# A decoder layer on eight cores: the last down pass by token quarters over a bf16 weight copy, four K heads first, and GpSimd work tied to a mask

## The chip, the cores and the metric

The kernel runs as one program on the 8 cores of one Trainium2 chip: cores 0 to 3 are one die, 4 to 7 the other. The metric is device time in microseconds (us) of the slowest core. Most runs of a kernel agree within 0.3%. Some runs fall into a slower state, in which one die or both get a lower TensorE clock; each run is labelled fast or slow, and only fast runs are compared here. The experiments ran on several chips, each beside the kernel before on the same chip.

Engine names in the profile: PE is TensorE, PEld its weight loads, DVE is VectorE, ACT is ScalarE, POOL is GpSimd, SP is SyncE. "L474" is line 474 of that kernel, so that one operation has different line numbers in different kernels.

## The reference, cut to what matters

One hybrid decoder layer, 16384 tokens, width 2048, float32 in and out:

```python
proj = x @ w_in + b_in                       # Q, K, V of group A; Q, K, V of group B
ya = dilated_mixture_attention(rope(qa), rope(ka), va)   # group A: 8 heads, three dilation patterns
yb = sink_window_attention(rope(qb), rope(kb), vb, sinks) # group B: 16 heads, 2 KV heads, window 128
y = concat([rms_norm(ya, g_a), rms_norm(yb, g_b)]) @ w_out
x = layer_norm(ALPHA * x + y, ln1_g, ln1_b)
x = layer_norm(ALPHA * x + (silu(gate) * up) @ w_down, ln2_g, ln2_b)   # d_ff = 5632
```

Each core computes 2048 tokens. It projects K and V for these tokens and the 2048 before them, stores them to memory, then projects Q and does the attention, then the rest.

## The kernel before

The phases follow each other on TensorE: K and V of eight x tiles of 512 tokens; Q and the attention of group B; that of group A; the output projection; and, for each half of 1024 tokens, an up pass and a down pass. Weights and x are loaded by GpSimd's DMA queue, which casts float32 to bf16. Three places matter here.

The start computes V of the first tile as its weights arrive, then V of the second tile, then K head by head. SyncE's queue loads the rope tables and V's bias at once, without a wait.

In the attention loops, VectorE's rope operations for later Q tiles stand in a queue (`dveq`, four to a tile), and `run(dveq, n)` puts n of them between the masks.

```python
for u in range(32):            # group B
    b_PV(j, kq, pend); b_evac(j, kq)
    run(peq, 1)
    proj(u + LEAD)             # the next Q projection, into one of two PSUM banks
    run(dveq, 4)               # its rope
    if u >= 29: reduce_b(u - 29)     # RMS statistics, into one of the same two banks
...
for u in range(32):            # group A
    for p_ in range(3):        # three dilation patterns
        spend.append(a_S(...)) # scores, exp (ScalarE), mask (VectorE)
        run(dveq, 2 if p_ == 0 else 1)
        a_PV(...)              # (cut: half of the next projection, before the third pattern's a_PV)
        if u >= 29 and p_ == 1: reduce_a(u - 29)   # needs acc of the block
    a_evac(h, c)               # output multiply (VectorE), copy and acc (GpSimd)
    proj(u + 32 + LEAD, 1)     # its other half
```

The down pass takes each weight tile for both token quarters of 512, so both sets of LayerNorm statistics are complete only at its end:

```python
for si in range(2 * KC):
    n, hh = si // 2, si % 2        # weight tile n, quarter hh
    ...                            # 44 matmuls, residual add, stats(n, hh, z, ...)
finish(0, 4); finish(1, 6)         # statistics of both quarters, then 32 tiles to normalise
```

The softmax here doesn't subtract the row's maximum and nothing guards it: scores larger than these inputs give would overflow.

Of the kernel before, what the change touches and what calls it, by code (L numbers as in the profile page):

```python
# [203 lines left out]
def build(debug=False):  # L204
# [15 lines left out]
    k.wk_d = ein("wk", [8, 128, KC, 128])  # L220
# [16 lines left out]
    k.rb_d = dt("rb", [128, TOK], F32, kind="Internal").ap()  # L237
    k.x1s_d = dt("x1s", [KC, 128, TOK], F32, kind="Internal").ap()
# [44 lines left out]
def persist(k):  # L283
    nc, S_ = k.nc, k.S
    P = Place(k, 0, 8192)
    k.perm, k.bperm = P("perm", 128)
    k.ones, k.bones = P("ones", 128)
    k.onh, k.bonh = P("onh", 128)
    k.onesf, k.bonesf = P("onesf", 128, F32)
    k.bqk, bs = P("bqk", 25, F32)  # L290
    k.bsmall = bs
    k.bsw, _ = P("bsw", 16, F32)
    k.gmix, _ = P("gmix", KC, F32)
    lnp, _ = P("lnp", 4 * KC, F32)
    k.lnp = lnp.rearrange("p (a b) -> p a b", a=4)
    k.esink, _ = P("esink", 8, F32)
    k.p_end = P.o
    S_.dma("pool", k.perm, k.perm_d, [], [k.bperm], "perm")
    for v, d in ((k.bqk, k.bqk_d), (k.bsw, k.bsw_d), (k.gmix, k.gmix_d), (k.lnp, k.lnp_d), (k.esink, k.sinks_d)):
        S_.dma("sp", v, d, [], [], "small", joins=[bs])  # L300
    S_.dve(lambda: nc.vector.memset(k.ones, 1.0), [], [k.bones])
    S_.dve(lambda: nc.vector.memset(k.onesf, 1.0), [], [k.bonesf])
    S_.act(lambda: nc.scalar.activation(out=k.esink, in_=k.esink, func=AF.Exp), [bs], [bs])
    S_.dve(lambda: nc.vector.tensor_scalar(out=k.gmix, in0=k.gmix, scalar1=32.0, scalar2=None, op0=ALU.mult), [bs], [bs])
# [46 lines left out]
def phase1(k):  # L351
# [9 lines left out]
    wk, bwk = [], []  # L361
    for h in range(8):
        v, b = P("wk%d" % h, KC * 128)
        wk.append(v.rearrange("p (a b) -> p a b", a=KC))
        bwk.append(b)
# [13 lines left out]
    ct = {"bk": 0, "t": 0, "ko": 0, "vo": 0}  # L379
# [21 lines left out]
    s0 = xs[slot_of[0]]  # L401
    bl0 = []
    kc = 0
    for p_ in (1, 1, 2, 4, 4, 4):
        o_ = XO + kc * 1024
        b_ = S_.buf("x0_%d" % kc, o_, o_ + p_ * 1024)
        S_.dma("pool", s0[:, kc:kc + p_, :], k.xT_d[0, :, kc:kc + p_, :], [], [b_], "x0_%d" % kc)
        bl0 += [b_] * p_
        for q in range(kc, kc + p_, 2):
            n_ = min(2, kc + p_ - q)  # L410
            for q_ in range(q, q + n_):
                S_.dma("pool", wv[:, q_, :], k.wv_d[q_], [], [bwv[q_]], "wv%d" % q_)
        kc += p_
    bx[0] = bl0
    S_.dma("sp", bv, k.bv_d[0], [], [bbv], "bv")
# [3 lines left out]
    load_x(1, (4, 4, 4, 4))  # L419
    for h in range(8):  # L420
        S_.dma("pool", wk[h], k.wk_d[h], [], [bwk[h]], "wk%d" % h)
    S_.dma("pool", wkb, k.wkb_d, [], [bwkb], "wkb")
# [38 lines left out]
    def k_tile(t, h):  # L461
        x = xs[slot_of[t]]
        bk = nx("bk", 8)
        ri = t % 2

        def mm():
            for kc in range(KC):
                ins = nc.tensor.matmul(bank(k, bk), wk[h][:, kc, :], x[:, kc, :], start=(kc == 0), stop=(kc == KC - 1))  # L468
            return ins
        S_.pe(mm, bx[t] + [bwk[h]], [k.bBK[bk]])  # L470
        flush()
        ti = nx("t", 2)
        ko, bko = KO[ki := nx("ko", 3)]
        rope_a(k, bk, h, ra[ri][:, 0, :], ra[ri][:, 1, :], bra[ri], T1[ti][0], T1[ti][1], T2[ti][0], T2[ti][1], ko, bko)  # L474
        b = Buf("ka%d_%d" % (h, t))
        S_.dma("sp", k.ka_d[h, t], ko, [bko], [b], "ko%d" % ki)
        k.bka[h].append(b)
# [25 lines left out]
    def load_ra(t):  # L503
        S_.dma("sp", ra[t % 2], k.ropeA_d[t], [], [bra[t % 2]], "ra%d" % (t % 2))

    load_ra(0)
    load_ra(1)
    x = xs[0]
    for kc in range(KC):
        def mm(kc=kc):  # L510
            for blk in range(4):
                for g in range(2):
                    ins = nc.tensor.matmul(bank(k, blk * 2 + g), x[:, kc, blk * 128:blk * 128 + 128],
                                           wv[:, kc, g * 512:g * 512 + 512], start=(kc == 0), stop=(kc == KC - 1))
            return ins
        S_.pe(mm, [bx[0][kc], bwv[kc]], k.bBK)
    for blk in range(4):
        v_out(0, blk, [(0, 512), (512, 1024)], [blk * 2, blk * 2 + 1])
    for blk in range(4):
        v_tile(1, blk)  # L520
    for h in range(8):
        k_tile(0, h)
    load_x(2, (8, 8))
    load_ra(2)
    for h in range(8):
        k_tile(1, h)
        if h == 0:
            load_x(3, (8, 8))
    load_ra(3)
# [28 lines left out]
def phase2(k):  # L558
# [312 lines left out]
    def a_evac(h, c):  # L871
# [9 lines left out]
        if h == 0:  # L881
            S_.pool(lambda: nc.gpsimd.tensor_tensor(out=ac, in0=yc, in1=yc, op=ALU.mult), [byc], [bacc[c]])
        else:
            S_.act(lambda: nc.scalar.activation(out=sq, in_=yc, func=AF.Square), [byc], [SQ[1]])
        if h < 7:
            y, by = YA[h % 2]
            if c == 0:
                open_gen(by)
            S_.pool(lambda: nc.gpsimd.tensor_copy(out=res(y), in_=ma(yc)), [byc], [], [by])
        else:  # L890
            for st in range(2):
                S_.pool(lambda st=st: nc.gpsimd.tensor_copy(out=res(k.y[st][:, 7, :]), in_=ma(yc)[:, 64 * st:64 * st + 64]), [byc],
                        [], k.by[st][7])
        if h > 0:
            eng, ve = ("dve", nc.vector) if (h, c) == (7, 3) else ("pool", nc.gpsimd)
            S_._add(eng, lambda: ve.tensor_tensor(out=ac, in0=ac, in1=sq, op=ALU.add), [SQ[1], bacc[c]], [bacc[c]])
        if c == 3 and h < 7:
            b = Buf("ys%d" % h)
            S_.dma("sp", k.ys_d[h], y, [by], [b], "ya")
            k.bys[h] = b  # L900

    rsum = []
# [31 lines left out]
    for u in range(32):  # L934
# [6 lines left out]
        run(peq, 1)  # L941
        proj(u + LEAD)
        run(dveq, 4)
# [6 lines left out]
    for u in range(32):  # L950
# [7 lines left out]
        if u == 28:  # L958
            k.y_load(0, 6)
            k.y_load(1, 6)  # L960
            wfill(k)
        for p_ in range(3):
# [4 lines left out]
            run(dveq, 2 if p_ == 0 else 1)  # L967
# [3 lines left out]
            if 28 <= u < 31:  # L971
                for _ in range(2):
                    if len(k.norms) > 48:
                        out_norm(k, *k.norms.pop(0))
            if u >= 29 and p_ == 1:
# [3 lines left out]
        a_evac(h, c)  # L979
        proj(u + 32 + LEAD, 1)  # L980
# [14 lines left out]
def out_open(k, rsum):  # L995
# [30 lines left out]
    for st in range(2):  # L1026
        k.wlist += [(("u", st, f), k.wup_d[f], KC * 256, KC, ((8192, 16384, 0) if st == 0 else (0, 16384, 8192))[f % 3]) for f in range(FC)]
        k.wlist += [(("d", st, n), k.wdn_d[n], FC * 128, FC, (0, 11264)[n % 2]) for n in range(KC)]
# [3 lines left out]
def wfill(k):  # L1032

    while k.wlist:
# [6 lines left out]
        k.S.dma("pool", v, src, [], [b], "ws")  # L1041
# [30 lines left out]
def phase3(k):  # L1072
# [128 lines left out]
    wdone(k, "xr")  # L1201
    hslots = list(range(32, 44)) + list(range(32))
    zr = {}
    bz2s = {}
    for st in range(2):
# [37 lines left out]
        zring = []  # L1243
        for si in range(2 * KC):
            n, hh = si // 2, si % 2
            if hh == 0:
                w, bw = k.wts[("d", st, n)]
# [13 lines left out]
            if hh == 1:  # L1261
                wdone(k, ("d", st, n))
# [3 lines left out]
                                                                          op1=ALU.add), [bxb, k.bBK[bk]], [bz])  # L1266
            stats(n, hh, z, bz, sqs)
# [4 lines left out]
            zr[(st, n, hh)] = (z, bz)  # L1272
        if st == 0:
            fins += [lambda: finish(0, 6), lambda: finish(1, 6)]
        else:
            finish(0, 4)
            finish(1, 6)

        def ln2_tile(st, n, hh, idx):
            c0 = st * TS + hh * 512  # L1280
            (mu, bmu), (rs, brs) = stat[hh]
            if st == 0:
                z, bz = slot("zl%d" % idx, R[0] + (4 + idx % 6) * 2048)
                S_.dma("sp", z, k.z2s_d[n, :, c0:c0 + 512], [bz2s[(n, hh)]], [bz], "zl%d" % (idx % 6))
            else:
                z, bz = zr[(st, n, hh)]
            eng = S_.dve
            e = nc.vector
            S_.dve(lambda: nc.vector.tensor_tensor(out=z, in0=z, in1=mu, op=ALU.subtract), [bz, bmu], [bz])  # L1289
            S_.dve(lambda: nc.vector.tensor_tensor(out=z, in0=z, in1=rs, op=ALU.mult), [bz, brs], [bz])  # L1290
            S_.act(lambda: nc.scalar.activation(out=z, in_=z, func=AF.Identity, bias=k.lnp[:, 3, n:n + 1], scale=k.lnp[:, 2, n:n + 1]),
                   [bz, k.bsmall], [bz])
            b = Buf("out%d_%d_%d" % (st, n, hh))
            final.append(S_.dma("act", k.outT_d[n, :, c0:c0 + 512], z, [bz], [b], "of%d" % (idx % 6)))

        for hh in range(2):
            for n in range(KC):
                jobs.append(lambda st=st, n=n, hh=hh, idx=hh * KC + n: ln2_tile(st, n, hh, idx))
# [37 lines left out]
def prepare_inputs(x, w_in, b_in, sinks, g_mix_a, g_mix_b, w_out, ln1_g, ln1_b, w_up, w_down, ln2_g, ln2_b):  # L1336
# [11 lines left out]
    wk = chunks(w_in[:, 1024:2048])  # L1348
# [24 lines left out]
    shared = dict(wq=wq, wk=wk, wkb=wkb, wv=wv, bqk=bqk, bsw=bsw, wout=wout, wup=wup, wdn=wdn, gmix=gmix, lnp=lnp,  # L1373
# [35 lines left out]
```

## Time and profile before

| | us |
|---|---|
| median of 4 runs (lowest to highest) | 3147.1 (3145.7 to 3152.4) |
| spans of the profiled run, by core | 3122.0 to 3137.1 |
| TensorE busy, slowest core | 2985.4 |

The profiled run took 3138.2 us, some 8 us less than the four timed ones.

To follow a change through such a kernel, the span is cut at instructions that stay the same. The stages below are read from the first and last TensorE start of certain lines; they are medians over the eight cores, and the last one is measured to the end of the span.

| stage | before, us |
|---|---|
| start, K and V, to the first Q projection | 514.7 |
| group B, to its first statistics matmul | 190.0 |
| to the last Q projection (most of group A) | 232.9 |
| to the first output projection (end of group A) | 50.2 |
| output projection | 238.8 |
| up, down, up (sum of the three) | 1542.9 |
| last down pass | 303.7 |
| tail after the last down matmul | 55.1 |

TensorE's waits before. The columns are: engine and line that waited, what ended the wait, us in total, number of waits, the longest.

```profile
PE sp L846 <- DVE arena L876: 32.5, 27, 3.9
PE sp L513 <- DMA arena<-wv: 21.5, 7, 9.4
PE sp L455 <- DMA arena<-xT: 9.9, 1, 9.9
```

The first line is group A: the next block's output matmuls wait for VectorE to multiply the block before (L876). The other two are the start: V's weights and the second x tile come too late.

TensorE's timeline of the start before, on core 5. The columns are start, us, engine, line, operation, and in brackets the idle time before it and what ended it.

```profile
67.45 30.04 PE L455 MATMUL sp<-arena 128*128 128x512 bf16 x128 [8.45 <-DMA arena<-xT]
97.32 55.42 PE L468 MATMUL sp<-arena 128*128 128x512 bf16 x256
152.57 27.79 PE L455 MATMUL sp<-arena 128*128 128x512 bf16 x128
180.20 27.79 PE L468 MATMUL sp<-arena 128*128 128x512 bf16 x128
```

Before 67.45 us there are another 128 matmuls. So 640 matmuls are done at 180.20. At the steady 0.216 us each (128 in 27.79 us), that is 138 us of work: 42 us are lost.

The end of TensorE's work before, on the slowest core, whose span ends at 3137.1: the last down matmuls end at 3082.6, and only statistics follow.

```profile
3059.78 22.83 PE L1258 MATMUL sp<-arena 128*128 128x512 bf16 x105
3082.44 1.88 PE L1115 MATMUL sp<-arena 128*128 128x512 f32 x4
```

### The profile page before, as it was taken

Reading aid. Unit: us, or ns where it says so; the run is one execution under the profiler, and the core shown is the slowest. Engines: PE = TensorE matmul, PEld = TensorE weight load, DVE = VectorE, ACT = ScalarE, POOL = GpSimd, SP = SyncE. Lnnn points to the kernel's source line nnn. Section 1 sums busy time; section 2 is a strip of 40 time slices with the busy share of each in tenths; the row PEclk is TensorE's granted clock in tenths of the full one; section 3 lists DMA queues with packets and bytes.
Section 4 is the critical chain, followed back from the end, with each engine's and each line's share of the span. In section 5 each row is a group of like instructions: output and inputs, shape, how many; then the busy total and the mean of one; then the engine's idle time right before and its main releaser. Section 6 shows DMA issues by size and latency. Waiting matters only on the chain.

```text
span 3137.1 us, 40048 instructions; the slowest of 8 cores (3122.0 to 3137.1 us)
## 1 busy us (share of the span) xinstructions
PE 2985.4 (95%) x15989; PEld 1423.7 (45%) x15989; DVE 1086.0 (35%) x1452; ACT 643.2 (21%) x889; POOL 594.4 (19%) x598
## 2 busy tenths in 40 slices
PE   5999999999997998999999999999999999999993
PEld 2445554545664443444444444444444444444441
DVE  0555545887776685421001000002420100100006
ACT  0000001665554133310000001112210000011114
POOL 2000000453323966000000002321000000012231
PEclk8999999999999999999999999999999999999997
DMA  9852213255557898754443446667954444445443
GB/s 171 158 120 87 79 52 78 41 124 132 120 132 188 166 195 166 149 102 78 81 76 73 81 86 128 135 128 147 215 106 78 81 72 76 81 85 108 103 104 111
DMA packets 186425, 352.36 MB, mean 112 GB/s; under 512 B 86400, under 2 KB 104064, under 8 KB 169344
## 3 DMA queue, kind: packets, MB, share of 16 engines
q0 software_dynamic: 31536, 190.13, 35.4%
q1 hardware_dynamic: 135696, 125.04, 14.7%
q10 hardware_dynamic: 19008, 34.61, 3.5%
q8 instruction: 129, 2.11, 0.3%
q14 instruction: 56, 0.46, 0.1%
HBM read 471.11 MB, written 68.75 MB: 172 GB/s over the span
## 4 chain that ended last, share of the span: by engine, by line
PE 81%; DVE 7%; DMA 5%; issue 3%; ACT 2%; POOL 1%; another core or an unknown queue 0%; DVEq 0%; ACTq 0%; SPq 0%; POOLq 0%
PE sp L1223 35%; PE sp L1258 19%; PE sp L468 7%; PE sp L455 7%; PE sp L692 4%; PE sp L1066 4%; DMA arena<-z2s 2%; DMA arena<-wv 1%; DMA outT<-arena 1%; DVE arena L655 1%; DVE arena L1130 1%; DVE arena L1290 1%; DVE arena L1289 1%; DVE arena L876 1%; ACT arena L826 1%
## 5 line engine op out<-in xcount | busy, mean ns | idle before, releaser
L1223 PE MATMUL sp<-arena 128*128 128x512 bf16 x5632 | 1223.1, 381 | 12.9 <-DVE arena L1231 7.6
L1223 PEld LDWEIGHTS sp<-arena 128*128 128x128 bf16 x5632 | 551.4, 98 | 685.7 <-issue 25.5
L1258 PE MATMUL sp<-arena 128*128 128x512 bf16 x2816 | 608.1, 379 | 2.2 <-ACT arena L1230 2.2
L1231 DVE TENSOR_TENSOR arena<-sp,arena 128x512 bf16<-128x512 f32 x176 | 121.6, 692 | 982.3 <-ACT arena L1230 982.3
L1258 PEld LDWEIGHTS sp<-arena 128*128 128x128 bf16 x2816 | 275.0, 98 | 335.3 <-issue 3.1
L1230 ACT ACTIVATE arena<-sp 128x512 f32<-128x512 f32 x176 | 105.0, 597 | 925.6 <-PE sp L1223 918.0
L127 POOL DMA_DIRECT2D arena<-wup x88 | 46.6, 530 | 1110.5 <-PE sp L1223 1077.5
L1265 DVE SCALAR_TENSOR_TENSOR arena<-arena,sp 128x512 f32<-128x512 f32 x64 | 44.0, 688 | 565.0 <-PE sp L1258 305.0
L692 PE MATMUL sp<-arena 128*128 128x512 bf16 x1024 | 235.5, 379 | 3.9 <-DVE arena L346 3.9
L1066 PE MATMUL sp<-arena 128*128 128x512 bf16 x1024 | 222.3, 379 | 5.6 <-DVE arena L1185 3.2
L1106 POOL TENSOR_TENSOR arena<-arena 128x512 f32<-128x512 f32 x120 | 158.4, 1320 | 350.3 <-DVE arena L1265 312.2
L455 PE MATMUL sp<-arena 128*128 128x384 bf16 (+1 forms) x1168 | 212.8, 345 | 9.9 <-DMA arena<-xT 9.9
L468 PE MATMUL sp<-arena 128*128 128x512 bf16 x1024 | 222.2, 379 | 0.0
L655 DVE TENSOR_TENSOR arena<-arena 128x1024 bf16<-128x1024 bf16 x160 | 144.3, 916 | 65.3 <-ACT arena L826 54.1
L455 PEld LDWEIGHTS sp<-arena 128*128 128x128 bf16 x1168 | 114.5, 98 | 106.9 <-issue 13.7
L1107 POOL TENSOR_TENSOR arena<-arena 128x512 f32<-128x512 f32 x120 | 160.2, 1335 | 0.0
L1066 PEld LDWEIGHTS sp<-arena 128*128 128x128 bf16 x1024 | 99.6, 98 | 128.4 <-issue 9.5
L468 PEld LDWEIGHTS sp<-arena 128*128 128x128 bf16 x1024 | 100.0, 98 | 120.5
L1105 ACT ACTIVATE arena<-arena 128x512 f32<-128x512 f32 x120 | 75.5, 629 | 363.0 <-DVE arena L1265 267.7
L692 PEld LDWEIGHTS sp<-arena 128*128 128x128 bf16 x1024 | 96.4, 98 | 113.4 <-issue 7.3
L340 ACT ACTIVATE arena<-sp,arena 128x512 bf16<-128x512 f32 (+1 forms) x37 | 25.1, 678 | 564.1 <-PE sp L488 443.6
L437 DVE TENSOR_TENSOR arena<-sp,arena 128x384 bf16<-128x384 f32 (+1 forms) x81 | 47.9, 605 | 200.5 <-PE sp L455 105.4
(102 smaller groups left out, 2012.9 us busy)
## 6 DMA issues: line engine op xcount, KB each, us to landing
arena<-wup POOLq DMA_DIRECT2D x88, 1024.0 KB, 9.0
arena<-wdn POOLq DMA_DIRECT2D x32, 1408.0 KB, 11.7
arena<-wout POOLq DMA_DIRECT2D x32, 512.0 KB, 10.1
arena<-xres SPq DMA_DIRECT2D x64, 256.0 KB, 8.0
x1s<-arena ACTq DMA_DIRECT2D x64, 256.0 KB, 7.7
arena<-x1s SPq DMA_DIRECT2D x64, 256.0 KB, 5.0
outT<-arena ACTq DMA_DIRECT2D x64, 256.0 KB, 4.0
arena<-xT POOLq DMA_DIRECT2D x12, 1024.0 KB, 21.9
```

Of the source, the lines that this page charges most:

```text
L455: ins = nc.tensor.matmul(bank(k, bk)[:, 0:c1 - c0], x[:, kc, blk * 128:blk * 128 + 128], wv[:, kc, c0:c1], start=(kc == 0), stop=(kc == KC ...
L468: ins = nc.tensor.matmul(bank(k, bk), wk[h][:, kc, :], x[:, kc, :], start=(kc == 0), stop=(kc == KC - 1))
L655: S_.dve(lambda: nc.vector.tensor_tensor(out=pg, in0=pg, in1=m.to_broadcast([128, rows, 1024 // rows]), op=ALU.mult), [bp, b], [bp])
L692: ins = nc.tensor.matmul(bank(k, bk), w[:, kc, :], x[:, kc, :], start=(kc == 0), stop=(kc == KC - 1))
L1066: ins = nc.tensor.matmul(bank(k, bk), w[:, kc, :], y[:, kc, hh * 512:(hh + 1) * 512], start=(first and i == 0), stop=(last and i == len(kc ...
L1105: S_.act(lambda: nc.scalar.activation(out=sq, in_=z, func=AF.Square), [bz], [bsq])
L1106: S_.pool(lambda: nc.gpsimd.tensor_tensor(out=za, in0=za, in1=z, op=ALU.add), [bz, bza], [bza])
L1107: S_.pool(lambda: nc.gpsimd.tensor_tensor(out=qa, in0=qa, in1=sq, op=ALU.add), [bsq, bqa], [bqa])
L1223: ins = nc.tensor.matmul(bank(k, a + half), w[:, kc, half * 128:half * 128 + 128], xb[:, kc, hh * 512:(hh + 1) * 512], start=(kc == 0), st ...
L1230: S_.act(lambda si=si, a=a: nc.scalar.activation(out=sg[si][0], in_=bank(k, a), func=AF.Silu), [k.bBK[a]], [sg[si][1]])
L1231: S_.dve(lambda si=si, a=a, f=f, hh=hh: nc.vector.tensor_tensor(out=h[f][:, hh * 512:(hh + 1) * 512], in0=bank(k, a + 1), in1=sg[si][0], o ...
L1258: ins = nc.tensor.matmul(bank(k, bk), w[:, fc, :], h[fc][:, hh * 512:(hh + 1) * 512], start=(fc == 0), stop=(fc == FC - 1))
```

## The change

It has three parts.

1. **Start.** K of four heads is computed first, for two x tiles at once, as x and weights arrive, filling all eight PSUM banks. ScalarE copies the banks into staging buffers so that they come free, and VectorE ropes from there. V follows. The rope tables and V's bias are loaded later, to leave the DMA engines to what comes first.
2. **Group A.** The last rope add moves behind the output multiply. GpSimd's copy and sum are held back until the next block's first mask is done. In group B, rope moves ahead of the next projection. With the last add, the third of the four rope operations moves too, from the second mask to the first.
3. **Down.** The first down pass stores each weight tile once as bf16. The last one goes by quarters, reading the bf16 copy twice, and normalises the first quarter under the second one's matmuls. A shorter end is split over three engines.

The diff, cut to its core (left out, among others: two loads of the output projection's input move one pattern later in block 28 of group A):

```diff
@@ start @@
+    for p_ in (1, 1, 2, 2, 2, 2, 2, 2, 2):        # x of tiles 0 and 1, K weights of four heads, in turn
+        ...
+    for h in range(4, 8): S_.dma("pool", wk[h], ...)
+    for kc in range(KC): S_.dma("pool", wv[:, kc, :], k.wv_d[kc], [], [bwv[kc]], "wv")
+    late = [bx[1][15]]
+    S_.dma("sp", bv, k.bv_d[0], [bwv[8]], [bbv], "bv")     # waits for the ninth part of V's weights
...
+    load_ra(0, late)                                       # rope tables: wait for the last x chunk
+    load_ra(1, late)
+    for kc in range(KC): ...                               # K of heads 0 to 3, tiles 0 and 1
+    for h in range(4):
+        for t in range(2): k_out(t, h, 2 * h + t)          # ScalarE staging, rope, store
@@ group B @@
+        run(dveq, 4)
         proj(u + LEAD)
-        run(dveq, 4)
@@ group A @@
-            run(dveq, 2 if p_ == 0 else 1)
+            if p_ == 0:
+                run(dveq, 3)
+                while poolq:
+                    poolq.pop(0)([spend[-1][1]])           # GpSimd waits for the mask just issued
...
         a_evac(h, c)                                       # now queues its GpSimd work in poolq
+        run(dveq, 1)
@@ down @@
-        for si in range(2 * KC):
-            n, hh = si // 2, si % 2
+        steps = [(n, hh) for n in range(KC) for hh in range(2)] if st == 0 else [(n, hh) for hh in range(2) for n in range(KC)]
+        for si, (n, hh) in enumerate(steps):
...
+            if st == 0 and hh == 0:
+                S_.dma("sp", k.wdb_d[n], w, [bw], [k.bwdb[n]], "wdb")
...
+            if st == 1 and si == 15:
+                fins.append(lambda: finish(0, 6))
+                jobs += [lambda n=n: ln2_tile(1, n, 0, n) for n in range(KC)]
```

## The prediction

> **What bounds it now.** TensorE is busy 2985 of 3137 us on the slowest core (page, part 1). The change goes at three of its gaps. (1) Start: in the timeline the first matmul is at 9.4 us, then it waits for V weights, then 9.9 us for the second x tile; at 68.4 us only 128 matmuls are done, 27.6 us of work at the steady 216 ns. 41 us are lost. (2) Group A (740 to 970 us): TensorE 205.7 of 230 us busy; the waits view gives 32.5 us in 27 waits to VectorE's output multiply. One block lasts 8.2 us. (3) Tail: the last down matmul ends at 3082.5; the remaining 54.5 us are statistics (about 6), 32 tiles on VectorE at 1.40 us, and the last store (2.7).
>
> **Tail.** By quarters, 16 tiles are normalised under the second quarter's matmuls. Left after the last matmul: z 0.9; four f32 matmuls, mean and variance to 5.7; table load 1.28, Ln and Exp to about 9; VectorE 17 passes of 0.69 beside GpSimd 11 of 1.27, to about 23; last ScalarE pass and store to about 28. Saved 26, less 2 for the first quarter's statistics matmuls, now in the TensorE stream: **-24 us**.
> Price: weights are stored once as bf16 (1.44 MB per 19 us, first down pass) and read twice. The DMA view there shows 16% of 16 engines moving 16.3 MB on the hardware queue, so about 4.3 us more per 19, at a share of 0.62 now: 0.84. No stall above a few us. In the second pass each 9.5 us step needs its own 1.44 MB. The skill's "DMA: Bandwidth & Descriptors" (Anatomy of one DMA) fits 2.0 us + bytes/436e3: 5.3 us; this trace has nothing as good (2 MB rope load: 11.4 us under contention). Estimate 6 to 8 us: no stall, little room.
>
> **Start.** K of four heads for two x tiles needs 12.6 MB for 128 matmuls; each 0.79 MB feeds 1.73 us of work. At the trace's rate, about 0.3 MB/us of f32 source, the first stage ends near 50, K of the other heads 78, V weights land near 95. Lost then about 28 instead of 41; ScalarE staging (0.65 per tile) frees the banks, VectorE's rope backlog (2.9 per tile) is absorbed. **-13 us** (8 to 18).
>
> **Group A.** The strided last rope add (1.06 us) stands before the output multiply on VectorE and delays it 0.45 us; it moves behind. Saved 0.4 in 26 blocks. The first mask lasts 1.33 to 1.42 instead of 0.69 while GpSimd copies; the skill ("SBUF — State Buffer", Who interferes with whom) says VectorE with two SBUF inputs contends with GpSimd reads. Tying GpSimd behind the mask restores 0.69, but TensorE rarely waits there (1.5 us). **-11 us**.
>
> **Sum.** 3147 - 48 = **3099 us**, range 3080 to 3122. Faster by over 2% (below 3084) 0.17, within 2% 0.82, slower 0.01.
>
> **Right if:** last down matmul to end 26 to 31 us; TensorE 99% busy in both down passes; first 512 matmuls end near 140, not 153.9 us; block period 7.7 to 7.9 us; first mask 0.69.
> **Wrong if:** bf16 loads land later than 9.5 us (gaps before down steps), bf16 stores delay x1 loads or weights in the first down pass, or V weights come late because K stores and rope tables share the DMA engines; better, if more of group A's 24 idle us goes.

## More of the kernel before

K and V go to memory through small output buffers:

```python
KO = [P("ko%d" % i, 512) for i in range(3)]       # K outputs: three buffers
VO = [P("vo%d" % i, VW) for i in range(2)]        # V outputs: two buffers
...
S_.dma("sp", bv, k.bv_d[0], [], [bbv], "bv")      # V's bias: waits for nothing
...                                               # (cut: load_ra(0), load_ra(1), x and weight loads)
for blk in range(4):
    v_tile(1, blk)
for h in range(8):
    k_tile(0, h)                                  # 16 matmuls, rope on VectorE, store on SyncE's queue
```

## The result, and the profile after

The kernel after is correct. Its median is 3184.95 us (3176.33 to 3190.48, four runs), against 3147.1: ratio 1.0115, 95% interval 1.0089 to 1.0141. A ratio is the mean time of one kernel's fast runs over that of the other's of the same rounds, so it is not quite the ratio of the medians quoted. A gain of 48 us had been predicted; 38 us were lost.

The cores come first, because a die that lost its clock must not be explained as a scheduling effect. The lines for the two dies, before and then after:

```profile
die 0 (median of its cores): 3130.2 us, clock 0.986
die 1 (median of its cores): 3128.2 us, clock 0.985
```

```profile
die 0 (median of its cores): 3157.1 us, clock 0.980
die 1 (median of its cores): 3178.7 us, clock 0.970
```

Die 0 is 27 us longer than before. Die 1 is another 22 us longer at a lower clock: it loses 11 us in the output projection and 6 to 7 us in the first down pass, where die 0 loses nothing. In the trace, cores 4 and 5 were granted a clock of 0.81 for 201 us in all, nearly all of it in short pieces after 1071 us, and cores 6 and 7 for 167 us; cores 0 to 3 never. So the schedule accounts for 27 us, and the rest is a question of clock (run e15 below).

Stages in medians over cores; the two columns on the right are runs of the experiments, which the text comes to.

| stage | before | after, die 0 | after again (e15) | best (e13) |
|---|---|---|---|---|
| start, K and V | 514.7 | 550.8 | 550.0 | 507.6 |
| group B to first statistics | 190.0 | 192.4 | 192.2 | 191.4 |
| to last Q projection | 232.9 | 237.3 | 236.2 | 228.1 |
| end of group A | 50.2 | 60.8 | 60.7 | 52.2 |
| output projection | 238.8 | 238.7 | 239.3 | 238.6 |
| last down pass | 303.7 | 305.4 | 305.4 | 305.4 |
| tail | 55.1 | 29.8 | 29.4 | 29.8 |

The tail gained 25 us as predicted. The start lost 36 us instead of gaining 13, and the group A edits lost 16 to 17 us in the three attention stages, instead of gaining 11.

TensorE's waits after:

```profile
PE sp L552 <- ACT arena L486: 34.4, 1, 34.4
PE sp L880 <- DVE arena L910: 22.5, 16, 5.2
PE sp L535 <- DMA arena<-wka: 19.2, 7, 8.7
PE sp L462 <- DVE arena L444: 9.9, 1, 9.9
PE sp L961 <- DVE arena L328: 7.1, 3, 2.7
PE sp L951 <- POOL arena L932: 6.8, 3, 3.1
```

Group A's known wait fell from 32.5 to 22.5 us (second line; medians over the cores 31.1 and 22.5), so that part of the reasoning worked. But four new waits stand there: one of 34.4 us for ScalarE's staging copy, one of 9.9 us for V's evacuation, and two sets of three in front of the statistics matmuls of group B (L961) and group A (L951).

The start after on core 5: first SyncE's queue, then VectorE's rope, then TensorE.

```profile
78.44 0.33 SPq L127 DMA_DIRECT2D arena<-bv  x1
78.86 1.21 SPq L127 DMA_DIRECT2D arena<-ropeA  x2
```

```profile
99.25 1.39 DVE L492 TENSOR_TENSOR arena<-arena 64x512 f32<-64x512 f32 x2 [88.58 <-DMA arena<-ropeA]
```

```profile
55.01 27.79 PE L474 MATMUL sp<-arena 128*128 128x512 bf16 x128 [1.10 <-ACT arena L486]
117.24 15.42 PE L552 MATMUL sp<-arena 128*128 128x512 bf16 x64 [34.44 <-ACT arena L486]
156.40 58.54 PE L462 MATMUL sp<-arena 128*128 128x512 bf16 x256 [9.94 <-DVE arena L444]
```

TensorE has 256 matmuls done at 82.8 us, where the kernel before had them at 97.3. The plan works up to there. Then it stands still: rope cannot start before 99.25, because the rope table's load was issued only at 78.86 and then took 20 us to land. It stood in SyncE's queue behind V's bias, which waits for a part of V's weights. Without rope, the eight staging buffers stay full, ScalarE can't empty PSUM, and TensorE has no bank. 640 matmuls are done at 214.9 us, 35 us later than before.

The tail after, on core 5, whose span ends at 3182.6: the last down matmuls end at 3153.8.

```profile
3129.79 23.98 PE L1366 MATMUL sp<-arena 128*128 128x512 bf16 x107
3153.61 1.88 PE L1283 MATMUL sp<-arena 128*128 128x512 f32 x4
```

The DMA view after, with KB each and the median us from issue to landing:

```profile
arena<-wdb SPq DMA_DIRECT2D x32, 1408.0 KB, 6.3
arena<-wdn POOLq DMA_DIRECT2D x16, 1408.0 KB, 13.8
wdb<-arena SPq DMA_DIRECT2D x16, 1408.0 KB, 12.5
```

A bf16 weight tile lands 6.3 us after its issue (the median), and TensorE consumes one in 9.5 us. In both down passes together TensorE waits 2.3 us.

### The profile page after: what moved, and what is told of

The parts are those of the page before. It is cut to its first block, busy times and chain, and to the rows that moved or that the text cites. A ratio compares the mean times of both kernels' runs of the same rounds, so it can differ in the third digit from the quotient of the medians.

```text
span 3182.6 us, 40219 instructions; the slowest of 8 cores (3147.1 to 3182.6 us)
## 1 busy us (share of the span) xinstructions
PE 3029.5 (95%) x15993; PEld 1438.0 (45%) x15993; DVE 1078.5 (34%) x1440; ACT 655.7 (21%) x907; POOL 619.6 (19%) x605
## 4 chain that ended last, share of the span: by engine, by line
PE 78%; DMA 10%; DVE 3%; ACT 3%; another core or an unknown queue 2%; issue 2%; POOL 1%; SPq 0%; ACTq 0%; DVEq 0%; POOLq 0%
PE sp L1332 36%; PE sp L1366 10%; PE sp L1120 7%; DMA arena<-x1s 7%; PE sp L462 7%; PE sp L474 5%; PE sp L726 5%; DMA arena<-z2s 1%; DMA arena<-ropeA 1%; PE sp L891 1%; ACT arena L1361 1%; DVE arena L1377 1%; DVE arena L910 1%; ACT arena L908 1%
## 5 line engine op out<-in xcount | busy, mean ns | idle before, releaser
L462 PE MATMUL sp<-arena 128*128 128x384 bf16 (+1 forms) x1232 | 227.4, 347 | 9.9 <-DVE arena L444 9.9
L689 DVE TENSOR_TENSOR arena<-arena 128x1024 bf16<-128x1024 bf16 x160 | 129.7, 836 | 61.3 <-ACT arena L860 45.5
L1361 ACT ACTIVATE arena<-arena 128x512 f32<-128x512 f32 x64 | 52.0, 813 | 362.3 <-DMA arena<-x1s 361.8
L1159 ACT ACTIVATE arena<-arena 128x512 f32<-128x512 f32 x119 | 74.9, 629 | 211.1 <-DVE arena L1377 108.0
```

Source lines behind the costliest of these rows:

```text
L462: ins = nc.tensor.matmul(bank(k, bk)[:, 0:c1 - c0], x[:, kc, blk * 128:blk * 128 + 128], wv[:, kc, c0:c1], start=(kc == 0), stop=(kc == KC ...
L689: S_.dve(lambda: nc.vector.tensor_tensor(out=pg, in0=pg, in1=m.to_broadcast([128, rows, 1024 // rows]), op=ALU.mult), [bp, b], [bp])
L1361: S_.act(lambda xb=xb, n=n: nc.scalar.activation(out=xb, in_=xb, func=AF.Identity, bias=k.lnp[:, 1, n:n + 1], scale=k.lnp[:, 0, n:n + 1]), ...
```

## The experiments

Fifteen experiments were run (e14 repeats the kernel of e10, e15 the kernel after). Some of them were executed only once or twice (e7, e8, e9, e12); those are read by their stages more than by their time.

### The start: is it only the position of V's bias? (e1, e2)

My theory was that the wait of V's bias on V's weights blocks everything behind it in SyncE's queue. The rival was that the DMA engines are simply full.

```diff
 # e1: V's bias behind the rope tables
-    S_.dma("sp", bv, k.bv_d[0], [bwv[8]], [bbv], "bv")
...
     load_ra(0, late)
     load_ra(1, late)
+    S_.dma("sp", bv, k.bv_d[0], [bwv[8]], [bbv], "bv")
 # e2: besides, load_ra(0) and load_ra(1) without the wait
```

> The changed kernel with one line moved: the load of the V bias stands after the two rope tables in SyncE's queue, not before. Theory (in-order queue: the rope tables stand behind the V bias, which waits for a V weight piece that lands only at 78 us): the tables are issued near 50 us, the 34 us wait of TensorE for the ScalarE staging falls to under 10, the first Q projection starts near 515 us instead of 550, the time is about 3150 (3140 to 3160). Rival (the 16 DMA engines are full of weights, so the tables land late wherever they stand): wait still over 20 us, time over 3168.

> The changed kernel with the rope tables loaded at the very start, waiting for nothing, and the V bias after them. In-order theory: no wait of TensorE for the staging is left, the first stage is at most 4 us later, the first Q projection starts at 498 to 508 us, the time is about 3138 (3128 to 3150). Bandwidth rival: the first stage gets slower by over 8 us and eats it, time as for the kernel with the bias last or more.

Measured: e1 has a start of 545.2 us and fast runs at 3160 to 3166; e2 has 545.5 us and fast runs at 3155 to 3180. Against what was expected, the start is 30 us too long in e1 and over 37 in e2. The first block was real: in e1 the tables land 10 and 14 us after their issue, and TensorE's wait for the staging copy falls from 34.4 to 7.6 us (core 5), as the theory said; so full DMA engines were not the main thing that held the tables. But taking the block away showed the next, a TensorE wait of 27.8 us for V's evacuation. SyncE's queue of e1 on core 5:

```profile
49.94 0.96 SPq L127 DMA_DIRECT2D arena<-ropeA  x2
83.37 0.33 SPq L127 DMA_DIRECT2D arena<-bv  x1
83.80 68.95 SPq L127 DMA_DIRECT2D ka<-arena  x16
```

The rope table now goes out at 49.94, but the K stores stand behind the bias and start at 83.80. VectorE fills the three K output buffers and then waits:

```profile
102.80 0.69 DVE L494 TENSOR_TENSOR arena<-arena 128x512 bf16<-128x512 f32 x1 [30.80 <-DMA ka<-arena]
```

The Trainium skill says why the order matters: in "DMA: Bandwidth & Descriptors" (Anatomy of one DMA), "DMA engines do not wait on semaphores"; a wait is done by the issuing sequencer before dispatch. The trace agrees: a queue whose head waited until 83.37 issued nothing behind it before.

### No wait in SyncE's queue at all, and more K buffers (e5, e6)

```diff
 # e5
-    load_ra(0, late); load_ra(1, late)
+    load_ra(0); load_ra(1)
+    S_.dma("sp", bv, k.bv_d[0], [], [bbv], "bv")
 # e6: e5, and K outputs of tiles 0 and 1 in sixteen buffers
+        if t < 2:
+            ki = 3 + nx("kx", 16)
+            ko, bko = KX[ki - 3]
```

> The changed kernel with rope tables and V bias loaded at the start, none waiting: SyncE's queue never blocks. The run with the bias last moved the block from the tables to the K stores (issued at 82 us, 20 us to landing, VectorE stands 31 us). If the queue order is all of it: K stores are issued from about 62 us, VectorE's ropes never stand over 5 us, first Q projection at 500 to 508 us, time about 3125 to 3138 on an undisturbed chip. If the stores themselves are slow while weights fill the 16 engines (20 us each, three output buffers, so 6.7 us a K tile against 3.45 on TensorE): waits of VectorE for K stores go on until about 100 us, TensorE still waits 10 us or more after the first V tiles, first Q projection at 515 to 535 us.

> As e5_sp_free, and each of the first 16 K tiles gets an output buffer of its own, so that no rope waits for a store. If slow stores with three buffers are what is left: VectorE ropes run through (2.95 us each, done near 110 us), TensorE waits for staging or V evacuation under 8 us, first Q projection at 498 to 508 us. If VectorE's rope work itself is too slow for a K-first order, it stays at 515 or more although no rope waits for a store.

Measured: e5 3144.3 us (3140.6 to 3160.6), ratio 1.0031 (0.9953 to 1.0108), start 528.0, as the second expectation had it (slow stores). e6 3144.8 us (the median of four, one of them slow), ratio 1.0011 (0.9979 to 1.0042), start 527.5. So the wait in the queue is worth 22 us of the 36. Sixteen K buffers alone add nothing, though rope now runs through to 109.8 us as expected, because the next thing in line is V. Of e6, core 3, VectorE's evacuation of V:

```profile
149.95 2.48 DVE L444 TENSOR_TENSOR arena<-sp,arena 128x512 bf16<-128x512 f32 x4 [37.77 <-DMA vs<-arena]
```

A V store of 256 KB, issued at 111, had its buffer free only 38 us later. Two rope tables stand just before it in the queue, but they are not the reason: in e13 below they are issued after these V stores, and the first of them still land 30 to 36 us after their issue. There are two V buffers, so VectorE and then TensorE (18.4 us in one wait) stand behind it. Over the window from 60 to 150 us the DMA view of core 5 shows, for K stores (the lines are of the kernel after, then of e5):

```profile
ka<-arena SPq DMA_DIRECT2D x14, 128.0 KB, 1.9
```

```profile
ka<-arena SPq DMA_DIRECT2D x16, 128.0 KB, 10.3
vs<-arena SPq DMA_DIRECT2D x2, 256.0 KB, 23.8
```

The same 128 KB store takes 1.9 us when most of the loads are through, as they were after the stall of the kernel after, and 10.3 us while they run. The skill's fit of 2.0 us plus bytes over 436e3 (same page, same section; made for GpSimd's queue) gives 2.3 us for it, an estimate. The trace is near it for the unloaded store; the other took more than four times as long.

### More V buffers (e9), and the same without the losses of group A (e10, e11)

```diff
 # e9: the rope tables, then the bias, wait for the last x chunk only; eight V buffers
-    S_.dma("sp", bv, k.bv_d[0], [bwv[8]], [bbv], "bv")
+    S_.dma("sp", bv, k.bv_d[0], late, [bbv], "bv")
-        vi = nx("vo", 2)
+        vi = 2 + nx("vx", 8) if t < 2 else nx("vo", 2)
     # and the rope tables of tiles 2 and 3 are loaded after V of tile 1
```

> The kernel after, with the rope tables and then the values' bias waiting only for the last chunk of the first x (not for the last part of the values' weights), with eight output buffers for the values of the first two row groups instead of two, and the third and fourth rope tables loaded later. Theory (small stores wait 20 to 40 us behind large loads, and too few output buffers hand that wait to VectorE and TensorE): the first K stage ends at about 54 us, TensorE waits under 6 us in all on VectorE's values evacuations, and the phase to the first Q projection lasts 500 to 511 us. Rival (the start is bound by the bytes that have to come in, whatever the order): 520 us or more, with TensorE's waits moved to weights or x. The rest of the kernel is as in the kernel after, so the whole time is about 3115 to 3130 us or 3145, respectively.

> The parts that the earlier runs showed to pay, alone: the last down pass over the bf16 copy, the moved last rope add and the first mask's GpSimd tie of group A, but group B's VectorE order as in the kernel before and GpSimd untied in the last five blocks; the start as in the kernel before. If the parts add: first B statistics to last Q projection 226 to 229 us (before 233), last Q to first out projection 50 to 52 us, tail 29 to 30 us, cores at 3098 to 3100 us undisturbed, time 3100 to 3113, ratio about 0.989. If group A's gain does not add (rival): as the down part alone, 3111 to 3114.

> The previous kernel with the repaired start (K of four heads first, staged by ScalarE, rope tables and bias not behind the values' weights, eight output buffers for the values). If the new start was only blocked by the queue and the buffers: phase to the first Q projection 500 to 511 us against 515, and 5 to 12 us below the previous kernel of the same rounds. If the start is bound by bytes: 515 to 528 us, and 0 to 13 us above it.

Measured: e9 has a start of 515.8 us, between both expectations: the loss is gone, and the gain has not come. It changes three things at once, so the 12 us against e5 are not put down to the V buffers alone. Its one fast run is 3128.1. e10 (down part and the good part of group A, old start) has two fast runs at 3110.3 and two slow ones. e11 (e10 with e9's start) has 3107.5 to 3110.4, ratio 0.9867 (0.9785 to 0.9948), start 515.1. The wide interval comes from runs of the kernel before at 3165 and 3175. Where the gain went is seen in TensorE's timeline of e11 on core 5:

```profile
58.07 27.79 PE L474 MATMUL sp<-arena 128*128 128x512 bf16 x128 [1.09 <-ACT arena L486]
122.32 57.95 PE L462 MATMUL sp<-arena 128*128 128x512 bf16 x256 [4.73 <-DVE arena L444]
180.11 27.79 PE L474 MATMUL sp<-arena 128*128 128x512 bf16 x128
```

Here 256 matmuls are done at 85.7 us, 11.6 us ahead of the kernel before (97.3). At matmul 640 nothing is left (180.11 against 180.20). In between, VectorE waited 14.9 us in eight waits for K stores with three buffers, so V's evacuation, which stands behind the rope, came late.

### Both kinds of buffers (e13), and the old start beside it (e14)

```diff
 # e13: e11 with
+    VX = [... for i in range(4)] + VO        # six V buffers for tiles 0 and 1, where e11 has eight
+    KX = [... for i in range(8)] + KO        # eleven K buffers for tiles 0 and 1
```

> The kernel of the repaired start, with eleven output buffers instead of three for K of the first two row groups, and six for the values. There the gain of 11.6 us at matmul 256 was gone at matmul 640, and between them VectorE waited 15 us for K stores, so that the values' evacuations began only at 121.5 us and TensorE waited 4.7 us and then ran some matmuls at half rate. If these waits are what gave the gain back: VectorE's rope chain ends near 106 us instead of 121, no wait for K stores, TensorE's values wait gone, phase to the first Q projection 504 to 510 us, time about 3101. If the V weights' arrival alone gave it back (rival): 513 to 517 us, time as the repaired start or the start of before, 3107 to 3110.

> The same kernel as e10_best, beside e13 on one chip: 3108 to 3112 us in fast runs, phase to the first Q projection 514 to 516 us, ratio to the kernel before about 0.989. It gives the interval that the first run with two fast executions could not.

Measured on one chip: e13's fast runs are 3102.4 and 3104.1 (two more were slow), ratio 0.989 (0.9872 to 0.9909); e14's five are 3110.5 to 3117.4, ratio 0.9924 (0.9911 to 0.9937). The start is 507.6 us against 515.2. e13, core 5:

```profile
54.63 27.79 PE L476 MATMUL sp<-arena 128*128 128x512 bf16 x128 [1.09 <-ACT arena L489]
102.15 69.23 PE L464 MATMUL sp<-arena 128*128 128x512 bf16 x320
171.22 27.79 PE L476 MATMUL sp<-arena 128*128 128x512 bf16 x128
```

VectorE's rope chain ends at 106.4 instead of 121.5, without a wait for K stores. TensorE runs 320 matmuls through without a stop, and 640 are done at 171.22: 9.0 us before the kernel before. This is the fastest kernel. V's weights still cost it something: of the 64 matmuls between 82 and 102 us, the last 20 come at the pace at which the weights land.

### Group A: take it out (e3), take each half of it back (e7, e8), keep only the rope add (e12)

```diff
 # e3: the kernel after without all edits to groups A and B
 # e7: the kernel after, group B's order as before
-        run(dveq, 4)
         proj(u + LEAD)
+        run(dveq, 4)
 # e8: the kernel after, GpSimd untied in the last five blocks
+        elif 4 * h + c >= 27:
+            tail()
 # e12: the kernel before, with the down part and the moved rope operations alone (run(dveq, 3), then 1)
```

> The changed kernel with everything in the attention loops put back as before. By the stage table of the two profiles (group A: from the last Q projection to the first output projection 50 to 61 us, B to A +2, A +4) the group A part costs about 17 us: time about 3167 (3158 to 3175). The prediction's view (it saves 11): 3195 or more. If the throttling of die 1 in the output projection comes from the long waits at the end of group A, its clock is back at 0.98 and over, and it is 3155 or less.

> The changed kernel with the rope work of group B's blocks back behind the projection that it belongs to. Theory: the delayed rope holds the projection's bank when the B statistics matmul needs it (TensorE waits 2 to 2.7 us three times and slows down). Then from the first statistics matmul to the last Q projection it takes 226 to 229 us instead of 237, and the three waits are gone. Rival (the GpSimd tie slows the first A blocks): 235 or more.

> The changed kernel with GpSimd's work of the last five blocks issued at once, as before. Theory: in the last blocks there is no projection to hide behind, and the tied GpSimd work makes TensorE's A statistics matmuls wait (6.8 us in three waits, then a low clock): last Q projection to first output projection 50 to 53 us instead of 61. Rival (the later loads of the last y rows, or the masks): 58 or more.

> The kernel before with the down part and only the moved last rope add of group A; GpSimd's work is released as in the kernel before. If the rope add is group A's whole gain, first B statistics to last Q projection lasts 226 to 228 us; if the tie of GpSimd to the first mask is needed for it, 230 us or more.

The two stages, in medians over cores (of e12 over die 0, since its die 1 had lost clock):

| kernel | first B statistics to last Q projection | end of group A |
|---|---|---|
| before | 232.9 | 50.2 |
| after again (e15) | 236.2 | 60.7 |
| e3, without group A's edits | 232.5 | 50.6 |
| e7, group B's order as before | 228.1 | 61.3 |
| e8, GpSimd untied at the end | 236.3 | 51.5 |
| e12, only the moved rope add | 228.3 | 50.8 |
| e14, rope add and tie, neither loss | 228.3 | 51.0 |

e3's fast runs are 3147.5 to 3152.0, below the expected 3158 to 3175. Its clocks are back at 0.98, but so are those of the kernel after in e15, so e3 says nothing about die 1. e7 and e8 are 3155.95 and 3155.6, one run each. The rows take the change apart. The moved rope operations gain 4 to 5 us. Tying GpSimd to the mask gains nothing that e12 does not have, not even a faster mask: the first mask of a block takes 1.35 us before (the median), 0.72 in e12 without the tie and 0.69 with it. Group B's new order costs 8 us (and 1.6 in the stage before: 192.2 against 190.6 in e7), and the tie at the end costs 9 us.

What these two cost is seen at the statistics matmuls. TensorE at the passage from B to A, core 5, first of the kernel after, then of e7:

```profile
741.18 1.82 PE L961 MATMUL sp<-arena 128*128 128x512 f32 x2 [1.96 <-DVE arena L328]
742.93 1.04 PE L766 MATMUL sp<-arena 64*128 64x256 bf16 x10
743.89 1.06 PE L785 MATMUL sp<-arena 128*64 128x256 bf16 x10
744.75 0.64 PE L800 MATMUL sp<-arena 128*64 128x512 bf16 x6
...
751.61 2.00 PE L961 MATMUL sp<-arena 128*128 128x512 f32 x2 [2.66 <-DVE arena L328]
...
755.19 0.63 PE L785 MATMUL sp<-arena 128*64 128x256 bf16 x10
```

```profile
740.19 1.02 PE L961 MATMUL sp<-arena 128*128 128x512 f32 x2
746.14 1.02 PE L961 MATMUL sp<-arena 128*128 128x512 f32 x2
```

L961 is `reduce_b`, and L328 is the third rope operation, the last that reads the bank. By the code, the statistics take one of the two projection banks. With rope ahead of the projection, each bank's rope comes one block later, so the bank is still held. In e7, with the old order, there is no wait.

The wait costs twice. The pair of statistics matmuls takes 1.82 to 2.00 us after it and 1.02 without it, and the ten matmuls of L785 take 1.06 us soon after the wait and 0.63 later. The trace's record of the granted clock shows why. For core 5 of the kernel after, then of e7: the stretch and its length in us, TensorE busy (matmuls), the granted clock, DMA share and GB/s.

```profile
738.00:741.40 3.40, 1.44 (x7) 1.00 0.00 0
741.50:744.80 3.30, 3.30 (x24) 0.50 0.00 0
```

```profile
741.50:744.80 3.30, 3.30 (x34) 1.00 0.21 79
```

The clock is halved for 3.41 us after each of the three waits, from 741.41, 751.65 and 761.89 us. In the 3.41 us before these times TensorE was busy for 42, 22 and 39%. All 14 halvings on this core follow such a stretch of 44% or less; two stretches as low (33 and 42%) were followed by none, and some matmul records may be missing. In "TensorE: Matmul & The Clock Gate" (Part 1) the skill tells of a TensorE clock that is halved after an idle window of about 3.4 us and comes back after as long a busy one. The trace agrees with the length, but no idle window was needed: waits of 1.96 and 2.66 us were enough here.

Both costs together make up the loss. In medians over the cores, TensorE has the halved clock for 10.2 us of the stage up to the last Q projection in e15 and for 3.4 in e7, and idles 15.3 and 10.9 us in it. Half of the 6.8 us and the 4.4 us of idle time come to 7.8 us, an estimate; measured 8.1.

At the end of group A, `reduce_a` (L951) needs GpSimd's sum, which was held back until the next mask. With the tie off there, e8 has no such wait on its list. The halved clock has its part here too: 23.9 us of the stage in e15, 13.7 in e8.

### The down part alone (e4)

The kernel before, with the down edits only.

> The kernel before with the down part alone: bf16 copy, quarters, short end. If the tail is worth what both profiles show (54.5 to 29 us, less 2 for the extra statistics): 3147 - 22 = 3125 (3117 to 3133), down passes 303.7 and 305.5 us on every core. If the bf16 traffic is what takes clock from die 1: its cores at 0.975 or less in the record, down passes near 310, time over 3135.

Measured: fast runs at 3111.1, 3114.2 and 3154.4 (in the last one cores 0 and 1 had a clock of 0.974 and 0.973, the other die 0.988 to 0.990), and the kernel before at 3138.9 and 3139.1 beside it. The tail is 29.9 us, the last down pass 305.4 (before 303.7), the clock 0.989. So the down part is worth about 25 us, and in the profiled run the bf16 traffic costs no clock.

### The kernel after once more, on another chip (e15)

> The changed kernel itself, word for word, on another chip. In its four runs of record one die ran at a granted clock of 0.97 and was 20 us longer than the other. If that is the chip's state of that hour: fast runs at 3150 to 3168 us, both dies within 10 us of each other, clocks 0.98 and above. If the change itself costs one die its clock: one die again at 0.97, about 3180 us.

Measured: fast runs at 3160.5, 3165.0 and 3171.5, ratio 1.0097 (1.0078 to 1.0117). Both dies have clocks of 0.978 to 0.983, spans 3149 to 3159, and the output projection lasts 239.3 us on both. So the change can run without the loss of 11 us on die 1. Its low clock in all four runs then came from that chip at that time, or from the change on that chip; this was not separated, for the four runs of the kernel before have no clocks on record, and the cause was not found. The loss against the kernel before is much the same in both places: the ratio is 1.0115 there and 1.0097 here, and the intervals overlap.

## Why the prediction was wrong

The prediction was 3099 us (3080 to 3122). Measured: 3184.95 at the time, and 3160 to 3171 with both dies undisturbed.

- **Tail: right.** Predicted -24, and 26 to 31 us from the last down matmul to the end; measured -25 and 29 to 30. The bf16 load was estimated at 6 to 8 us and took 6.3 (the skill's fit, which is made for GpSimd's queue and not for SyncE's, gave 5.3). The down pass grew by 1.7 us, where 2 were predicted for the statistics in TensorE's stream.
- **Start: the step that failed.** It was "ScalarE staging frees the banks, VectorE's rope backlog is absorbed", for -13; measured +36. The arrival of K's x and weights was costed well (first stage to end near 50 us, measured 53.5 to 59; K of the other heads near 78, measured 82 to 88). But the prediction never followed SyncE's queue, where a load that waits for V's weights stands ahead of the rope table and of all stores. Staging moves a wait; it takes none away unless the consumer runs. The sentence "or V weights come late because K stores and rope tables share the DMA engines" named the right neighbours and the wrong direction: the stores were late, not the weights, whose last part landed at 95.4 us in the kernel after, where 95 was predicted (partly luck: the stores were held back, and in e13, where they are not, it is 101).
- **Start: the size, had it not been blocked.** Predicted loss 28 us instead of 41; e13 loses 33 instead of 42. The first stage ended at 53.5 us and not near 50, and the last of V's weights landed at about 101 there and not near 95. And this took eleven K buffers and six V buffers, which the change did not have.
- **Group A: the gain was over-sized, and two costs were missed.** Predicted -11, as 0.4 us in each of 26 blocks; the moved rope operations alone give 4 to 5 us. The term that was mis-sized is the saving in a block: in blocks 1 to 25 the mean distance of the output multiplies fell from 8.30 to 8.14 us (e12), by 0.16. Two blocks in four went from 8.2 to 8.3 us down to 7.85, as predicted; the others only from 8.24 to 8.08 and from 8.68 to 8.60. What holds these was not found. Group B's new order (+8) and the delayed GpSimd sum at the end (+9) were in the diff, and the prediction did not ask who waits for them. The mask's restored speed was real (0.69 us for the first mask, and from 916 to 828 ns in the mean over the masks from 500 to 970 us), but e12 has it without the tie (815 ns): the moved rope operations are enough for it. What it is worth by itself was not measured.
- **Die 1's clock** added some 20 us to the measured time, though hardly to the ratio. The profile before shows no such stretch of 0.81.

## What to carry to other kernels

In these runs a load that waits delayed all that stood behind it in its queue: before moving one, list what is issued after it and who needs that first. If large loads fill the DMA engines, a small store took five times as long and more here; count the output buffers by that time and not by the time of an idle store. When an operation is delayed on purpose on an idle engine, look for its last consumer at the ends of the loop, where no slack of a next block covers it.

## What the Trainium skill lacked or had wrong

- "DMA: Bandwidth & Descriptors" (Anatomy of one DMA) gives a time for one DMA. It has no figure for a small store among full loads: here 128 KB took 1.9 us in the median with most loads through, 10.3 us while loads filled the engines, and a 256 KB store 24 to 38 us.
- The same page says that waits are done by the issuing sequencer, but not the consequence: one waiting load in a queue holds all later, unrelated transfers. It held a rope table from about 50 to 79 us, and in the next experiment the K stores from about 63 to 84.
- "TensorE: Matmul & The Clock Gate" (Part 1) gives an idle window of about 3.4 us for the slower clock. Here the clock was halved after stretches of 3.41 us in which TensorE was busy for 22 to 42%, with waits of 1.96 and 2.66 us. A later passage there tells of short idle times that make the clock swing, but gives no share of busy time; the 14 halvings of one core here follow shares of 0 to 44%.
- "SBUF — State Buffer" (Who interferes with whom) is borne out: in the kernel before, masks on VectorE that run beside a GpSimd operation take 1.38 us in the mean, the others 0.71. A new order on VectorE alone, without any tie on GpSimd (e12), took the first mask out of its way: 0.72 us instead of 1.35.
